# Block sums of the down weights: GpSimd adds in SBUF in place of transfers in DRAM, and two products of a quarter exchanged

## The chip, the core and the metric

One core of a Trainium2 chip runs the whole program. The metric is the device time of one execution in microseconds, taken as the median of three runs. TensorE does the matmuls, VectorE and ScalarE the elementwise work, GpSimd some elementwise work and some transfers, and SyncE issues most loads.

## The reference

A decoder trunk of two layers on 512 tokens of width 1024, in float32. Layer A has sparse attention with compressed, selected and windowed branches and a cross-attention to 256 memory rows; layer B has dilated window attention over keys and values made once from layer A's output, and the same cross-attention. Each layer ends in an MLP, and it is in the two MLPs that the change lies:

```python
def squared_relu_mlp(h, w_up, w_down):            # (512,1024) x (1024,4096) x (4096,1024)
    return jnp.square(jax.nn.relu(h @ w_up)) @ w_down
...
y = y + squared_relu_mlp(rmsnorm(y, mlp_norm[l]), w_up[l], w_down[l])
```

## The kernel before

**Number format.** Every weight block is loaded into a buffer `st` (three of them, 128x1024) and split into a high and a low part in a buffer `w` (four of them): ScalarE copies the high part, VectorE subtracts it from the block. `mm3` then multiplies in three matmuls: high by high, high by low, low by high. `wload` is load and split together.

**The MLP.** `mlp(l)` is called for layer A (l = 0) and layer B (l = 1). The 4096 hidden columns are worked in four quarters `q` of eight 128-column tiles. In the up part, tile by tile, a weight tile is loaded and split, 24 matmuls of 512 columns make the hidden tile in PSUM, ScalarE takes relu and square, and the result is split into `a[j]`. After every second tile `combos` makes, on VectorE, sums and differences of the two tiles' row halves. In the down part the quarter's product with `w_down` is done in seven products in place of eight, by a scheme of block sums (two row halves, two halves of the hidden columns, two column halves of 512). A quarter of `w_down` has four blocks `B[0]` to `B[3]`, each of two half blocks of 128x1024. The products need these stationary sides and weights, in this order:

- X: `a[0..3]`, first rows, with `B[0]`; the sum over quarters of X is kept in `G`.
- Z: a combination, with `T[1]` = B1 + B3; then `into` adds it to the output rows.
- Y: `s2`, with `T[2]` = B0 + B1 + B3; added to `G`.
- Z again, accumulated in the same PSUM banks: `a[4..7]`, last rows, with `T[3]` = B0 + B1 + B2 + B3; `into`.
- V: `s1`, with `T[0]` = B0 + B1; `into`.
- X again, accumulated: `a[4..7]`, first rows, with `B[2]`; `into`.
- V again, accumulated: `s4`, with `B[3]`; `into`.

Each product fills two PSUM banks, in 24 matmuls: for each half block h, six into bank 0, then six into bank 1. `into` reads both banks on VectorE (one operation each), scales by the row's norm factor and adds to the output tile `xn`.

**The sums.** `T[0..3]` lie in DRAM. `blocks` is a generator whose steps issue, for one quarter after the other, four copies of blocks to DRAM tiles from ScalarE's queue, and four accumulating transfers on top of them from GpSimd's queue:

```python
for o, i in ((0, 0), (1, 1), (2, 3), (3, 2)):
    self.behind(self.nc.scalar.dma_start(t[o], b[i]))
    yield
for o, x in ((0, b[1]), (1, b[3]), (2, t[0]), (3, t[2])):
    self.behind(self.nc.gpsimd.dma_start(t[o], x, accum_op=ALU.add, max_dma_last_dim=4096))
```

`behind` makes each of them wait for an earlier marked operation, so that it does not start too soon. The steps for the first quarter are taken during layer A's attention (`paced`, one step every 13 ticks, from the twelfth item on); those of each later quarter during the up part of the quarter before it (`PM`). `product` then loads the half blocks of the sums like any other weight.

**Order.** The program is written as one stream; the framework lists the instructions of every engine in an order that it works out itself from when their inputs and buffers should be ready, and each engine then runs its list in order. A buffer that is taken again waits for the last reader of what it held.

At the end of layer A's MLP (`q` = 3, l = 0) `done` and `columns` square and transpose finished parts of the output while the last products run, and layer B starts with the projection to shared keys and values.

Of the kernel before, what the change touches and what calls it, by code (L numbers as in the profile page):

```python
# [14 lines left out]
P = 128  # L15
# [39 lines left out]


PA = 13
PM = (0, 0, 1, 1, 2, 3, 4, 6)
# [72 lines left out]
def paced(gen, n):  # L131

    while True:
        for _ in range(n):
            yield
        next(gen, None)


# [39 lines left out]
class K:  # L178
    def __init__(self, ctx, tc, ins, out):
        self.tc, self.nc, self.ins, self.out = tc, tc.nc, ins, out  # L180
        ps = lambda n, b: ctx.enter_context(tc.tile_pool(name=n, bufs=b, space=bass.MemoryType.PSUM))
        sb = lambda n, b: ctx.enter_context(tc.tile_pool(name=n, bufs=b))
        self.pacc, self.pS, self.pT, self.pO = ps("acc", 2), ps("ps", 3), ps("pt", 2), ps("po", 1)
        self.one = sb("one", 1)
        self.sb = sb("sb", 1)
        self.dram = ctx.enter_context(tc.tile_pool(name="dram", bufs=1, space=bass.MemoryType.DRAM))
        self.n = 0
        self.ev = 3
        self.staged = []
        self.sums, self.marks = {}, []  # L190
        self.adds, self.far = self.blocks(), 5
        self.lab = "s"
# [3 lines left out]
        cs=2, stt=4, vcb=1, ab=1,  # L196
# [13 lines left out]

    def marked(self, f):

        return lambda *a, **k: self.marks.append(f(*a, **k))  # L213
# [432 lines left out]
    def soft(self, Sp, nb, n):  # L646

        nc = self.nc
        nm = self.t("nm", [P, nb])
        sm = self.t("su", [P, nb])  # L650
        nc.vector.tensor_reduce(out=nm, in_=Sp, axis=AX.X, op=ALU.max, negate=True)
        p = self.t("p2", [P, nb, n])
        for b in range(nb):
            self.marked(nc.scalar.activation)(
                p[:, b, :], Sp[:, b, :], AF.Exp, bias=nm[:, b : b + 1], accum_out=sm[:, b : b + 1]
            )
        return p, sm
# [43 lines left out]
    def layer_a(self):  # L701
# [52 lines left out]
        slow = Work()  # L754
        slow.add(paced(self.adds, PA), None, lambda: len(seen) >= 12)
        attend(items, work, slow, RA, seen)
# [128 lines left out]
    def cmp_scores(self, g, q4, cmp, gt):  # L885
# [4 lines left out]
        VCB = self.t("vcb", [P, 2, P])  # L890
# [45 lines left out]
    def attn_a(self, g, ga, gt, cmp, out):  # L936
# [20 lines left out]
        def front(pr, half, hp, ii):  # L957
# [31 lines left out]
            for br in range(2):  # L989
                self.marked(nc.scalar.activation)(p[br], Sb[br], AF.Exp, bias=nms[br], accum_out=sm[:, br : br + 1])  # L990
# [81 lines left out]
    def behind(self, i):  # L1072

        self.tc.add_manual_dep(
            i.ins, self.marks[-self.far].ins.name, mybir.DependencyInfo(mybir.DependencyClass.Sync, mybir.DependencyReason.DATA),
            reason="start of a transfer",
        )

    def blocks(self):


        for l in range(2):
            for q in range(4):
                b = [self.ins["w_db"][l, q, i].rearrange("h p c -> (h p) c") for i in range(4)]
                t = [self.dram.tile([2 * P, D], F32, name=f"sum{l}{q}_{i}") for i in range(4)]
                for o, i in ((0, 0), (1, 1), (2, 3), (3, 2)):
                    self.behind(self.nc.scalar.dma_start(t[o], b[i]))
                    yield
                for o, x in ((0, b[1]), (1, b[3]), (2, t[0]), (3, t[2])):
                    self.behind(self.nc.gpsimd.dma_start(t[o], x, accum_op=ALU.add, max_dma_last_dim=4096))  # L1090
                    if o == 3:
                        self.sums[l, q] = t
                    yield
# [24 lines left out]
    def mlp(self, l):  # L1118
# [5 lines left out]
        self.far = 1  # L1124
# [74 lines left out]
        for q in range(4):  # L1199
            a, A12, A4 = [None] * 8, [], []  # L1200
            for n in range(8):
# [12 lines left out]
                self.marked(nc.scalar.activation)(u, ps, AF.Relu)  # L1214
# [12 lines left out]
                for _ in range(PM.count(n)):  # L1227
                    next(self.adds, None)

            def product(banks, stat, wsrc, again=False):  # L1230

                for h in range(2):
                    w = self.wload(wsrc[h])
                    for u in range(2):
                        for i in range(2):
# [5 lines left out]
                            )  # L1241
            blk = lambda k0, c0: lambda k: [a[k + k0][:, z, c0 : c0 + H] for z in (0, 1)]
# [3 lines left out]
            B = [ins["w_db"][l, q, i] for i in range(4)]  # L1246
            while (l, q) not in self.sums:
                next(self.adds)
            T = [t.rearrange("(h p) c -> h p c", h=2) for t in self.sums[l, q]]
            two = lambda pool: [self.ps(pool, [P, S]) for _ in range(2)]  # L1250

            def into(src, rows, cols, neg=False):

                for u in range(2):
                    b = 2 * rows + u
                    o = xn[b][:, cols * 512 : (cols + 1) * 512]
                    self.marked(nc.vector.scalar_tensor_tensor)(
# [6 lines left out]
            product(X, blk(0, 0), B[0])  # L1264
# [17 lines left out]
            product(Z, blk(4, H), T[3], True)  # L1282
# [4 lines left out]
            product(V, s1, T[0])  # L1287
# [16 lines left out]
            if last:  # L1304
                done(0, 1)
                if l == 0:
                    columns(0, 1)
# [121 lines left out]
    def attn_b(self, sp, q4, kv, oT, side):  # L1429
# [6 lines left out]
        def front(s, w, ih):  # L1436
# [43 lines left out]
            for ii in range(2):  # L1480
                n = sizes[ii]
                self.marked(nc.scalar.activation)(
# [241 lines left out]
```

## Time and profile before

| | |
|---|---|
| time, median of 3 runs | 1336.94 us (1335.43 to 1343.63) |
| the profiled execution | 1338.41 us, its span 1336.6 us |
| busy: TensorE, its weight loads | 1270.1 us (95%), 1044.9 us (78%) |
| busy: VectorE, ScalarE, GpSimd | 861.6 (64%), 774.7 (58%), 378.2 us (28%) |
| instructions | 18572 |
| moved by DMA | 214.23 MB, mean 160 GB/s |
| accumulating transfers from GpSimd | 32 of 1024 KB, medians 13.5 and 9.6 us to landing |
| mean granted TensorE clock | 0.981 of 2.4 GHz |

The span runs from the first to the last instruction of the profiled execution. Busy time counts an instruction from its start to its end; matmuls are pipelined and overlap, so a TensorE that is busy all the time is one that never stood without a matmul in flight.

### The profile page before, as it was taken

The page shows a single profiled execution, that of the slowest core. Times are in us where ns is not written, and L with a number is a line of the kernel's source. Part 1 is how long each engine was busy: PE and PEld are TensorE (multiplying, and loading weights), DVE is VectorE, ACT ScalarE, POOL GpSimd, SP SyncE. Part 2 cuts the span into 40 slices and gives each one's busy share as a digit, 9 for nine tenths or more (in the row PEclk, how much of TensorE's full clock was granted, in tenths as well). Part 3 has the DMA queues.
Part 4 walks back from the last instruction along what each step waited for, and adds up shares of the span by engine and source line. Part 5 has one row for each costly group of instructions (what it writes and reads, how often), then busy time and mean ns, then how long its engine had stood idle before and what let it go on. Part 6 is the DMA issues. An engine that isn't in the chain of part 4 may idle for free.

```text
span 1336.6 us, 18572 instructions
## 1 busy us (share of the span) xinstructions
PE 1270.1 (95%) x6465; PEld 1044.9 (78%) x6465; DVE 861.6 (64%) x1599; ACT 774.7 (58%) x1709; POOL 378.2 (28%) x481
## 2 busy tenths in 40 slices
PE   8868999999999999999999989989899999999998
PEld 6757787667688888888887878877668888888887
DVE  5976677755366756557478567666666655747556
ACT  6755467686376445463557547766757546455452
POOL 2444584554231000010001878572424001000000
PEclk9887999999999999999998999999999999999999
DMA  7224122333369688796976241211228879798534
GB/s 235 79 88 144 54 74 96 87 75 85 111 198 260 213 278 238 239 245 225 277 211 202 79 131 48 64 40 44 79 87 248 237 223 265 223 273 233 157 110 157
DMA packets 61261, 214.23 MB, mean 160 GB/s; under 512 B 6672, under 2 KB 13840, under 8 KB 60656
## 3 DMA queue, kind: packets, MB, share of 16 engines
q1 hardware_dynamic: 50224, 142.67, 32.8%
q0 software_dynamic: 9344, 35.77, 13.6%
q10 hardware_dynamic: 1600, 34.61, 7.2%
q8 instruction: 51, 0.84, 0.2%
q14 instruction: 42, 0.34, 0.1%
HBM read 207.78 MB, written 72.35 MB: 210 GB/s over the span
## 4 chain that ended last, share of the span: by engine, by line
PE 76%; DVE 8%; ACT 7%; DMA 4%; issue 3%; POOL 1%; ACTq 0%; SPq 0%; POOLq 0%; DVEq 0%
PE s_ps L250 14%; PE s_ps L252 14%; PE s_ps L251 13%; PE s_acc L250 5%; PE s_acc L251 5%; PE s_acc L252 5%; PE s_pt L252 3%; PE s_pt L251 3%; PE s_pt L250 3%; PE s_po L1030 2%; DMA s_st<-in_w_ao_dram 2%; ACT s_p L213 2%; ACT s_w L243 2%; DVE s_w L245 1%; DMA s_st<-in_w_ag_dram 1%
## 5 line engine op out<-in xcount | busy, mean ns | idle before, releaser
L245 DVE TENSOR_TENSOR s_w<-s_st,s_w 128x1024 fp32r<-128x1024 f32 (+3 forms) x240 | 285.4, 1193 | 274.2 <-ACT s_w L243 273.3
L243 ACT ACTIVATE s_w<-s_st 128x1024 fp32r<-128x1024 f32 (+4 forms) x272 | 263.5, 973 | 212.9 <-PE s_pt L252 51.7
L250 PE MATMUL s_ps<-s_act,s_w 128*128 128x512 f32 x576 | 225.4, 393 | 1.1 <-ACT s_act L285 0.7
L252 PE MATMUL s_ps<-s_act,s_w 128*128 128x512 f32 x576 | 225.0, 391 | 0.0
L251 PE MATMUL s_ps<-s_act,s_w 128*128 128x512 f32 x576 | 224.9, 390 | 0.0
L250 PEld LDWEIGHTS s_ps<-s_act,s_w 128*128 128x128 f32 x576 | 108.0, 188 | 25.9 <-ACT s_act L285 1.6
L252 PEld LDWEIGHTS s_ps<-s_act,s_w 128*128 128x128 f32 x576 | 108.1, 188 | 23.8 <-issue 1.6
L251 PEld LDWEIGHTS s_ps<-s_act,s_w 128*128 128x128 f32 x576 | 108.1, 188 | 23.1 <-issue 0.8
L250 PE MATMUL s_acc<-s_w,s_act 128*128 128x512 f32 (+3 forms) x304 | 110.3, 366 | 12.7 <-ACT s_w L243 9.0
L251 PE MATMUL s_acc<-s_w,s_act 128*128 128x512 f32 (+3 forms) x304 | 109.4, 360 | 1.4 <-DVE s_w L245 1.3
L252 PE MATMUL s_acc<-s_w,s_act 128*128 128x512 f32 (+3 forms) x304 | 106.9, 356 | 0.0
L213 ACT ACTIVATE s_p<-s_ps 128x512 f32<-128x512 f32 x64 | 38.2, 597 | 110.9 <-PE s_ps L252 110.9
L1090 POOL DMA_DIRECT2D sum<-in_w_db_dram x16 | 14.4, 900 | 302.6 <-ACT s_p L213 299.1
L660 POOL TENSOR_SCALAR s_p<-s_p,s_cr 128x256 f32<-128x256 f32 (+3 forms) x128 | 69.9, 568 | 89.7 <-DVE s_cr L601 24.1
L250 PEld LDWEIGHTS s_acc<-s_w,s_act 128*128 128x128 f32 x304 | 59.0, 195 | 20.8 <-ACT s_w L243 9.3
L245 POOL TENSOR_TENSOR s_w<-s_st,s_w 128x512 fp32r<-128x512 f32 (+4 forms) x32 | 53.2, 1666 | 74.9 <-ACT s_w L243 74.9
L213 ACT ACTIVATE s_p<-s_ps,s_nm 128x256 f32<-128x256 f32 (+3 forms) x128 | 65.4, 521 | 8.2 <-DVE s_nm L972 3.8
L251 PEld LDWEIGHTS s_acc<-s_w,s_act 128*128 128x128 f32 x304 | 59.0, 194 | 7.4 <-DVE s_w L245 3.1
L252 PEld LDWEIGHTS s_acc<-s_w,s_act 128*128 128x128 f32 x304 | 58.9, 194 | 4.5 <-issue 0.2
L668 ACT ACTIVATE s_pt<-s_pt 128x512 f32<-128x512 f32 (+2 forms) x101 | 52.4, 526 | 15.4 <-PE s_pt L1011 5.7
L285 ACT ACTIVATE s_qk<-s_p 128x256 fp32r<-128x256 f32 (+1 forms) x96 | 46.9, 489 | 23.1 <-DVE s_p L1100 21.1
L1090 POOL DMA_DIRECT2D sum<-sum x16 | 14.1, 882 | 140.6 <-issue 43.4
(334 smaller groups left out, 2971.2 us busy)
## 6 DMA issues: line engine op xcount, KB each, us to landing
s_st<-in_w_up_dram SPq DMA_DIRECT2D x64, 512.0 KB, 4.1
s_st<-sum SPq DMA_DIRECT2D x64, 512.0 KB, 6.2
s_st<-in_w_db_dram SPq DMA_DIRECT2D x48, 512.0 KB, 4.4
sum<-in_w_db_dram POOLq DMA_DIRECT2D x16, 1024.0 KB, 13.5
sum<-sum POOLq DMA_DIRECT2D x16, 1024.0 KB, 9.6
s_st<-in_w_bq_dram SPq DMA_DIRECT2D x16, 384.0 KB, 3.2
s_st<-in_w_ag_dram SPq DMA_DIRECT2D x11, 512.0 KB, 4.4
s_st<-in_w_c_dram SPq DMA_DIRECT2D x8, 512.0 KB, 4.0
```

The source lines that it names most:

```text
L213: return lambda *a, **k: self.marks.append(f(*a, **k))
L243: nc.scalar.activation(w[:, 0], st, AF.Copy)
L245: e.tensor_tensor(out=w[:, 1], in0=st, in1=w[:, 0], op=ALU.subtract)
L250: mm(ps, lh[0], rh[0], start=start, stop=False, skip_group_check=again)
L251: mm(ps, lh[0], rh[1], start=False, stop=False, skip_group_check=again)
L252: mm(ps, lh[1], rh[0], start=False, stop=stop, skip_group_check=again)
L285: nc.scalar.activation(dst[:, 0], src, AF.Copy)
L660: self.nc.gpsimd.tensor_scalar(out=p, in0=p, scalar1=c, scalar2=1.0, op0=ALU.mult, op1=ALU.mult)
L668: self.nc.scalar.activation(dst, src, AF.Copy)
L1030: nc.tensor.matmul(O[x * 64 : x * 64 + 64, q0 + o : q0 + 256], v[:, j, br, :], st[x][br][:, j, o:256], start=half == 0 and br == 0 and j = ...
L1090: self.behind(self.nc.gpsimd.dma_start(t[o], x, accum_op=ALU.add, max_dma_last_dim=4096))
```

## The change

The sums are made in SBUF. At the start of a quarter block 1 is loaded as four 128x512 tiles `U`. After the sixth and seventh hidden tile GpSimd adds block 3, loaded into `st`, to `U` and puts the result into four tiles `T` (buffers named `x`). Then, with the products: `w11` loads and splits block 0 for the first product, and GpSimd adds block 0 to `U` in place; `w3` splits `T` for Z, and GpSimd adds block 0 to `T`; `w2` splits `T` for Y, and GpSimd adds block 2, loaded for it, to `T`; `w4` and `w1` split `T` and `U`; the last two products load blocks 3 and 2 again. A split of `T` or `U` is made in two pieces of 512 columns (`wpieces`), where one of 1024 was made. The DRAM tiles, their transfers, the marks and the pacing go. The last two products change places: V again (`s4` with block 3) comes before X again (block 2), and with them their `into`, `done` and `columns`. A small tile of the attention (`vcb`, one buffer) takes a buffer of the tag `ki` (two).

```diff
-    def behind(self, i):
...
-    def blocks(self):
...
+    def addto(self, out, a, b):
+
+        for i, (o, x) in enumerate(zip(out, a)):
+            self.nc.gpsimd.tensor_tensor(out=o, in0=x, in1=b[:, i * 512 : (i + 1) * 512], op=ALU.add)
+
+    def wpieces(self, t):
+
+        w = self.t("w", [P, 2, 2 * 512], F32R)
+        for i in range(2):
+            self.wsplit(w[:, :, i * 512 : (i + 1) * 512], t[i], "v")
+        return w
...
+            B = [ins["w_db"][l, q, i] for i in range(4)]
+            U, T = [], []
             for n in range(8):
...
-                for _ in range(PM.count(n)):
-                    next(self.adds, None)
...
+                if n < 2:
+
+                    for i in range(2):
+                        U.append(self.t(("qki", "tq")[i], [P, 512]))
+                        nc.sync.dma_start(U[-1], B[1][n][:, i * 512 : (i + 1) * 512])
+                if n in (5, 6):
+
+                    t = [self.t("x", [P, 512]) for _ in range(2)]
+                    self.addto(t, U[2 * n - 10 : 2 * n - 8], self.wdma(B[3][n - 5]))
+                    T += t
...
+            b11 = []
+
+            def w11(h):
+
+                st = self.wdma(B[0][h])
+                b11.append(st)
+                w = self.t("w", [P, 2, 2 * 512], F32R)
+                self.wsplit(w, st, "v")
+                u = U[2 * h : 2 * h + 2]
+                self.addto(u, u, st)
+                return w
+
+            def w3(h):
+
+                t = T[2 * h : 2 * h + 2]
+                w = self.wpieces(t)
+                self.addto(t, t, b11[h])
+                return w
+
+            def w2(h):
+
+                t = T[2 * h : 2 * h + 2]
+                w = self.wpieces(t)
+                self.addto(t, t, self.wdma(B[2][h]))
+                return w
+
+            w4 = lambda h: self.wpieces(T[2 * h : 2 * h + 2])
+            w1 = lambda h: self.wpieces(U[2 * h : 2 * h + 2])
+            w21 = lambda h: self.wload(B[2][h])
+            w22 = lambda h: self.wload(B[3][h])
...
-            product(X, blk(0, 0), B[0])
+            product(X, blk(0, 0), w11)
...
-            product(Z, blk(0, H), T[1])
+            product(Z, blk(0, H), w3)
...
-            product(Y, s2, T[2])
+            product(Y, s2, w2)
...
-            product(Z, blk(4, H), T[3], True)
+            product(Z, blk(4, H), w4, True)
...
-            product(V, s1, T[0])
+            product(V, s1, w1)
...
-            product(X, blk(4, 0), B[2], True)
+            product(V, s4, w22, True)
             if last and l == 0:
                 columns(1, 1)
                 columns_end(1)
+            into(V, 0, 1)
+            if last:
+                done(0, 1)
+            product(X, blk(4, 0), w21, True)
+            if last and l == 0:
+                columns(0, 1)
             into(X, 0, 0)
...
-            product(V, s4, B[3], True)
-            if last and l == 0:
-                columns(0, 0)
-            into(V, 0, 1)
...
```

## Rows read from the trace of the kernel before

**Rows 1.** Stages: window, length, PE, PEld, DVE, ACT, POOL busy (x), clock, DMA share, GB/s.

```profile
150.00:320.00 170.00, 159.50 (x1007) 125.83 (x1007) 119.09 (x318) 122.59 (x370) 99.01 (x139) 1.00 0.29 81
...
362.00:690.00 328.00, 328.00 (x1464) 269.98 (x1463) 202.37 (x292) 175.19 (x258) 28.50 (x27) 1.00 0.81 238
690.00:730.00 40.00, 36.98 (x167) 30.23 (x166) 37.04 (x70) 27.67 (x59) 0.00 (x0) 0.91 0.69 221
```

**Rows 2.** TensorE in order of time, first matmuls of X and of X again.

```profile
512.42 0.39 PE L250 MATMUL s_acc<-s_w,s_qk 128*128 128x512 f32 x1
...
539.62 0.39 PE L250 MATMUL s_acc<-s_w,s_qk 128*128 128x512 f32 x1
```

**Rows 3.** Waits of one quarter's products: total us, times, longest.

```profile
ACT s_w L243 <- PE s_pt L252: 9.0, 6, 1.7
...
ACT s_w L243 <- DMA s_st<-sum: 3.0, 1, 3.0
```

**Rows 4.** VectorE by line and form, the products of one quarter.

```profile
L245 DVE TENSOR_TENSOR s_w<-s_st,s_w 128x1024 fp32r<-128x1024 f32 x14 | 17.0, 1222 | 12.4 <-ACT s_w L243 12.3
L213 DVE SCALAR_TENSOR_TENSOR s_pt<-s_pt,r,s_pt 128x512 f32<-128x512 f32 x4 | 2.8, 742 | 0.0
...
L1100 DVE TENSOR_TENSOR s_p<-s_p,s_p 128x256 f32<-128x256 f32 x3 | 1.3, 418 | 0.0
```

**Rows 5.** VectorE in order of time, the same quarter.

```profile
514.20 1.23 DVE L245 TENSOR_TENSOR s_w<-s_st,s_w 128x1024 fp32r<-128x1024 f32 x1 [3.88 <-ACT s_w L243]
...
523.94 1.22 DVE L245 TENSOR_TENSOR s_w<-s_st,s_w 128x1024 fp32r<-128x1024 f32 x1 [1.84 <-ACT s_w L243]
...
526.40 2.35 DVE L245 TENSOR_TENSOR s_w<-s_st,s_w 128x1024 fp32r<-128x1024 f32 x2
...
538.19 1.23 DVE L245 TENSOR_TENSOR s_w<-s_st,s_w 128x1024 fp32r<-128x1024 f32 x1 [1.46 <-ACT s_w L243]
539.33 1.40 DVE L213 SCALAR_TENSOR_TENSOR s_pt<-s_pt,r,s_pt 128x512 f32<-128x512 f32 x2
```

**Rows 6.** Issues for the sums: queue, count, min/median/max ns.

```profile
L1087 ACTq DMA_DIRECT2D sum<-in_w_db_dram x32: 496/497/610, 159.5 to 1181.7; - x32
...
L1090 POOL DMA_DIRECT2D sum<-sum x16: 869/878/930, 287.6 to 1214.6; - x16
```

**Rows 7.** GpSimd in order of time, late in attention A.

```profile
321.29 0.91 POOL L1090 DMA_DIRECT2D sum<-sum  x1
321.93 1.24 POOL L660 TENSOR_SCALAR s_p<-s_p,s_cr 128x256 f32<-128x256 f32 x2
```

**Rows 8.** Line 441, the adds of squares: min/median/max ns.

```profile
L441 POOL TENSOR_TENSOR s_raw<-s_raw,s_p x14: 1288/1351/2210, 392.7 to 1021.8; 128x512 f32<-128x512 f32 x14
L441 DVE TENSOR_TENSOR s_raw<-s_raw,s_p x7: 684/686/689, 11.4 to 22.6; 128x512 f32<-128x512 f32 x7
```

**Rows 9.** GpSimd in order of time, first MLP.

```profile
392.71 11.48 POOL L441 TENSOR_TENSOR s_raw<-s_raw,s_p 128x512 f32<-128x512 f32 x7
```

**Rows 10.** VectorE in order of time, the same stretch.

```profile
401.54 1.51 DVE L1100 TENSOR_TENSOR s_p<-s_p 128x256 f32<-128x256 f32 x1
...
405.00 0.41 DVE L1100 TENSOR_TENSOR s_p<-s_p,s_p 128x256 f32<-128x256 f32 x1
```

**Rows 11.** All engines in order of time, attention A.

```profile
162.66 1.23 DVE L245 TENSOR_TENSOR s_w<-s_st,s_w 128x1024 fp32r<-128x1024 f32 x1 [0.75 <-ACT s_w L243]
162.68 1.66 POOL L503 TENSOR_TENSOR s_tq<-s_tq,s_rb 128x192 f32<-128x192 f32 x1
...
164.00 0.55 DVE L984 TENSOR_REDUCE s_nm<-s_ps 128x1 f32<-128x384 f32 x1
...
164.30 0.60 POOL L504 TENSOR_TENSOR s_tq<-s_tq,s_rb 128x192 f32<-128x192 f32 x1
```

**Rows 12.** Busy time by stage, end of the first MLP; columns as in rows 1.

```profile
714.00:718.00 4.00, 2.57 (x16) 2.00 (x14) 3.73 (x9) 3.97 (x10) 0.00 (x0) 1.00 0.95 309
718.00:722.00 4.00, 2.41 (x9) 1.93 (x10) 4.00 (x7) 4.00 (x10) 0.00 (x0) 0.60 0.61 192
```

More of the change, by code (lines that the diff above doesn't have):

```diff
@@ L128, in __init__ @@
         self.front, self.back, self.args, self.seg, self.need = front, back, args, seg, need
[L131 to L136, printed above, removed]
 def attend(items, work, side, ratios, seen, lag=1):
@@ L189, in __init__ @@
         self.staged = []
-        self.sums, self.marks = {}, []
-        self.adds, self.far = self.blocks(), 5
         self.lab = "s"
@@ L195 @@
         act=12, st=3, w=4, qk=8, pt4=4, p2=6, raw=2, tmp=4, sq=1, rb=1, tq=2, qki=2, ki=2, x=8, r1=1, r2=1, r3=1, r4=2, r5=2, r6=3, r7=2, nm=6, su=5, cr=6, c1=2, c2=2, nb=4,
-        cs=2, stt=4, vcb=1, ab=1,
+        cs=2, stt=4, ab=1,
     )
@@ L753, in layer_a @@
         items = spread(L[0], C[0], 8, 0) + spread(L[1], C[1], 1, 1) + spread(L[2], C[2], 1, 1) + M
-        slow = Work()
-        slow.add(paced(self.adds, PA), None, lambda: len(seen) >= 12)
-        attend(items, work, slow, RA, seen)
+        attend(items, work, Work(), RA, seen)
         while work.step() is not END:
@@ L889, in cmp_scores @@
         KC, vc = cmp["KC"], cmp["vc"]
-        VCB = self.t("vcb", [P, 2, P])
+        VCB = self.t("ki", [P, 2, P])
         nc.gpsimd.memset(VCB, 0.0)
@@ L1069, in outpart @@
             nc.vector.tensor_tensor(out=self.x[m], in0=ps, in1=xo, op=ALU.add)
-    def behind(self, i):
[L1074 to L1077, printed above, removed]
-    def blocks(self):
[L1082 to L1093, printed above, removed]
+    def addto(self, out, a, b):
[6 more added lines that the diff above has]
+        return w
     def combos(self, u1, u2, a1):
@@ L1226, in mlp, with product @@
                     r, nr = inverse()
-                for _ in range(PM.count(n)):
-                    next(self.adds, None)
-            def product(banks, stat, wsrc, again=False):
+                if n < 2:
[6 more added lines that the diff above has]
+                    T += t
+            def product(banks, stat, weights, again=False):
                 for h in range(2):
-                    w = self.wload(wsrc[h])
+                    w = weights(h)
                     for u in range(2):
@@ L1245, in mlp @@
             s4 = lambda k: [A4[k][:, z] for z in (0, 1)]
[L1246 to L1249, printed above, removed]
             two = lambda pool: [self.ps(pool, [P, S]) for _ in range(2)]
@@ L1299, in mlp @@
                 done(0, 0)
-            product(V, s4, B[3], True)
-            if last and l == 0:
-                columns(0, 0)
-            into(V, 0, 1)
-            if last:
-                done(0, 1)
                 if l == 0:
-                    columns(0, 1)
+                    columns(0, 0)
                     columns_end(0)
```

15 lines of the change are left out of this document (5 added, 10 removed).

## The prediction

> **What bounds the kernel now.** I read the totals of the page first (TensorE is the busiest engine by far), then busy time by stage, then one quarter of an MLP instruction by instruction. By stage [rows 1], the first MLP from 362 to 690 us has TensorE busy 328.00 of 328 us at granted clock 1.00, with the DMA engines at 0.81; the attention stretch from 150 to 320 us leaves TensorE 10.5 us idle, and the join of the first MLP to layer B (690 to 730) leaves 3.0 us. So in an MLP the end is set by the matmuls alone. Five products there take 539.62 - 512.42 = 27.20 us [rows 2], 5.44 each, 24 matmuls at 0.2267 us. A quarter has 8 x 24 + 7 x 24 = 360 of them, 81.6 us; eight quarters are 653 us, half of the kernel. The change keeps every one of these matmuls. It can therefore win only outside the MLPs, and it can lose wherever TensorE is made to wait.
>
> What protects TensorE now is prefetch: the split of a block (a copy on ScalarE, a subtract on VectorE) waits mostly for a free w buffer, that is for TensorE itself (9.0 us in total), and only once for a sum from DRAM (3.0 us), which TensorE did not feel [rows 3]. With four w buffers the split for half-product k may start when k-4 ends. Count halves of 2.72 us from 512.42: half 6 (first half of the fourth product) is due at 512.42 + 16.32 = 528.74, and its subtract begins at 523.94 and takes 1.22, so it is 3.6 us early; half 7 is due at 531.46, its subtract ends about 527.6, 3.9 us early [rows 4, 5].
>
> **What is removed.** Per quarter four DRAM copies issued by ScalarE (0.50 us of its queue each) and four accumulating transfers issued by GpSimd (0.88 each) [rows 6], the loads of four sums (eight half blocks) and all of that traffic. In the MLPs this is worth nothing: TensorE never waits there [rows 1], so the DMA relief only lengthens the lead of the loads. The first quarter's sums are issued inside attention A: four issues on each queue, at most 4 x 0.50 + 4 x 0.9 = 5.6 us of queue time that exponentials or scalings of p could wait behind. One of the GpSimd issues visibly stands in front of the scaling of a block of p (321.29, then the scaling at 321.93) [rows 7]. Bound 0 to -5.6 us; I take -2, about a third, since both engines also idle in that stretch.
>
> **Loads.** SyncE now issues 12 half blocks a quarter where it issued 14: block 1 as four loads of half the size, then blocks 3, 0, 2, 3, 2. Two of the three st buffers hold block 0 until it has been added to T, and the third holds block 2, so the loads for the last two products queue on SyncE behind those adds. The tenth half is due at 512.42 + 27.2 = 539.6, far behind adds that should end near 525: cost nothing, covered by two products of TensorE. Buffers named ki in place of vcb: nothing, one memset.
>
> **The adds.** Each quarter has 16 adds of 128x512 on GpSimd. The same operation stands in the trace: 1.29 us at least, 1.35 median, against 0.686 on VectorE [rows 8]; seven in a row took 11.48 us, 1.64 each, with VectorE at work [rows 9]. 16 x 1.35 = 21.6 us fits in 81.6. The price is on VectorE: while GpSimd adds, a VectorE operation on two SBUF inputs waits for the add in progress. A 128x256 subtract takes 1.51 us in that run and 0.41 after it [rows 10], +1.1 each; in the other direction a 1024-wide subtract holds an add until it ends (a 192-wide add took 1.66, the next one 0.60), while a VectorE read of PSUM beside GpSimd keeps its usual time [rows 11]. The Trainium skill says the same (GPSIMD Engine Reference, § 1 Specifications: the SBUF interfaces are shared, with contention for VectorE instructions with two SBUF inputs), and its § 4.1 Engine selection advises against GpSimd for two-input elementwise work. The trace agrees on both; taken as a rule on this change, it is the second case below.
>
> Ten of the 16 adds (B1+B3, block 0 into U, and block 0 into the first half of T) fall in the up part or in the 3.88 us that VectorE idles ahead of 514.20 [rows 5]; there a w serves 24 matmuls, 5.44 us, and the delay is covered: nothing. The other six follow one another between 514.2 and 527.6: T+B0 for the second half, then T+B2 for both. Each needs the split of the old T by ScalarE and VectorE, and the next split needs the add. VectorE has in that stretch five subtracts of 1.22 and the combos (0.42 each) [rows 4], all on two SBUF inputs. Middle: six adds delay VectorE by 1.1 each, 6.6; less its idle of 1.84 in front of 523.94 [rows 5] and the 3.9 of lead, 0.9 us of waiting for TensorE per quarter. Lower bound 0 (the adds meet the PSUM reads instead: the adds of G and the into operations). Upper bound: each add costs its whole 1.35, so 8.1 - 1.84 - 3.9 = 2.4. I take the middle, since the 1.1 was measured on these very shapes: 8 x 0.9 = +7.2 us, bounds 0 to +19. Splitting T in two 512-wide pieces adds a fixed part of about 0.14 per half, inside that bound.
>
> **The exchange.** V = s1 product is now followed at once by the s4 product into the same two PSUM banks, so its first matmul waits until VectorE has read bank 0; before, the X product lay between. In the trace the V product ends at 539.62 [rows 2]. VectorE is then in the subtract that began at 538.19, and the two reads follow from 539.33, 1.40 for both [rows 5], 0.742 for one [rows 4]: bank 0 is free at 540.07, 0.45 late. Bank 1 is free at 540.73 and needed at 539.62 + 0.45 + 1.36 = 541.4: no second wait. Queued behind the reads on VectorE is the next subtract, which has 3 us of lead. 8 x 0.45 = +3.6 us; bounds 0 (the read goes ahead of the subtract) and 0.8 (the subtract begins just before), so 0 to +6.4. At the end of the first MLP, where VectorE is busy 37.04 of 40 us [rows 1], it may be 1 us more; the order of the last columns only changes places.
>
> **Sum.** -2 + 7.2 + 3.6 = +8.8. The profiled execution took 1338.41 us (span 1336.6 and 1.8 around it), 1.5 above the median of the three runs, 1336.94. 1338.41 + 8.8 = 1347.2; on the median 1345.7, so I say 1346.
>
> **The cases.** A change of less than 1% (13.4 us) is what a measurement of this kernel can hardly tell from none.
> - Forecast, 0.50: short waits in the products, 1338 to 1350.
> - The exclusion of GpSimd and VectorE sets the pace, 0.30: the chain split, add, split falls behind in every quarter. It decides once the quarter waits more than (13.4 + 2) / 8 = 1.9 us. At 2.4 + 0.45 it gives 8 x 2.85 - 2 = +20.8, 1358. For it: VectorE and the adds together have little idle in that stretch, and VectorE runs in order, so a piece that queues behind combos delays its add too. Against it: 3.6 to 3.9 us of lead. A lower clock could add to it: after TensorE had been busy only 2.57 of 4 us and then 2.41, the granted clock was 0.60 [rows 12]; waits of one microsecond did not bring that about inside an MLP, which shows none, so this stays unpriced beyond the range.
> - The adds hide completely and attention gains, 0.17: 1336.94 - 5.6 + 0 to 3.6, so 1331 to 1338. For it: VectorE is busy 202.37 of 328 us in the MLP [rows 1]. Against it: the reads at 539.33.
> - The instruction lists come out in another order, so that the adds to U fall into the product stretch too, and the change does not take the sums off the path: 4 x 1.35 more there, which is the second case and is in its chance.
> - Faster by over 1%, 0.03: it would need more than all of the 10.5 us idle in attention A.
>
> The bounds reach from 1336.94 - 5.6 = 1331 to 1336.94 + 19 + 6.4 = 1362; less the outer tenth on either side, 1333 to 1359. Slower by over 1%: 0.30; faster: 0.03; within: 0.67.
>
> **What would show it.** Right: in the MLP stages TensorE busy below the stage's length, its waits put down to VectorE's subtract (or ScalarE's copy) of w in the third and fourth product, and to the reads of V once a quarter; 256-wide VectorE operations of 1.5 us beside GpSimd adds; the quarter 82.5 to 83.5 us long. Wrong: a quarter of 81.6 us (the adds hidden, and the read ahead of the subtract), or waits of several microseconds at one place, above all for a load behind a held st buffer. A longer or shorter attention stage by more than 5 us would mean that the order of its instructions changed, which I have not priced.

## The result and the profile after

The changed kernel takes 1352.9 us (median of 4 executions, 1349.32 to 1357.2) beside 1336.87 for the kernel before: ratio 1.0111, 95% interval 1.0066 to 1.0156. The forecast was 1346 with a range of 1333 to 1359. So the time lies inside the range, above the likeliest case (1338 to 1350), and its median is just past the 1% that I had called hardly measurable, in the part that had 0.30. The profiled execution took 1349.32 us (span 1347.2).

Where the time went is read from stage lengths. A quarter of an MLP begins with the first Relu on ScalarE; the difference of two such starts is the length of a quarter. First quarter of the first MLP, in ScalarE's order of time, kernel before:

```profile
390.83 0.60 ACT L213 ACTIVATE s_p<-s_ps 128x512 f32<-128x512 f32 x1 [0.33 <-PE s_ps L252]
...
474.54 0.60 ACT L213 ACTIVATE s_p<-s_ps 128x512 f32<-128x512 f32 x1 [4.38 <-PE s_ps L252]
```

and after (line numbers have moved: the Relu is L1184, the split of a block L225 on ScalarE and L227 on VectorE, the split of activations L267 and L270, the combos L1069, the new adds L1055, reads of a product L1262, a product's three matmuls L232 to L234):

```profile
391.28 0.60 ACT L1184 ACTIVATE s_p<-s_ps 128x512 f32<-128x512 f32 x1 [0.33 <-PE s_ps L234]
...
479.07 0.60 ACT L1184 ACTIVATE s_p<-s_ps 128x512 f32<-128x512 f32 x1 [4.37 <-PE s_ps L234]
```

That quarter took 83.71 before and 87.79 after. In this way for all stages (us; A is from the start to the first Relu of the first MLP, B from its last quarter's first Relu through layer B to the second MLP's, so that the first MLP's last quarter lies in B; q0 to q2 are the first three quarters, of the first and then of the second MLP; "end" is the last quarter to the end of the span, which is read to 0.1 us; below the first row stand the differences to it, of one profiled execution each):

| kernel | A | q0 | q1 | q2 | B | q0 | q1 | q2 | end |
|---|---|---|---|---|---|---|---|---|---|
| before | 390.83 | 83.71 | 81.60 | 81.60 | 372.06 | 83.71 | 81.60 | 81.60 | 79.89 |
| after | +0.45 | +4.08 | +0.23 | +0.24 | -1.66 | +3.29 | +0.19 | +0.18 | +3.60 |
| e1 exchange alone | -1.34 | 0 | 0 | 0 | +4.59 | -0.01 | 0 | 0 | +0.26 |
| e2 no adds | +2.18 | -0.01 | 0 | 0 | +1.18 | 0 | 0 | 0 | +0.25 |
| e3 adds on VectorE | +1.33 | 0 | +0.89 | +1.06 | +4.73 | -0.01 | +1.04 | +1.02 | +4.34 |
| e4 before plus adds | -2.08 | +4.15 | +2.80 | +2.80 | +5.01 | +4.28 | +3.74 | +3.44 | +1.26 |
| e5 old order | +3.89 | +4.18 | +0.23 | +0.23 | +3.72 | +3.26 | +0.22 | +0.19 | +0.18 |
| e6 fewer held loads | +0.04 | +2.72 | +3.88 | +4.03 | +6.49 | +2.55 | +3.15 | +3.90 | +6.04 |
| e7 squares on VectorE | +1.24 | -0.12 | +0.22 | +0.23 | +3.37 | -0.11 | +0.19 | +0.20 | +3.58 |
| e8 no sums in attention | +4.04 | -0.01 | 0 | 0 | -4.61 | 0 | 0 | 0 | +0.28 |
| e9 e5 and e7 | +3.51 | -0.11 | +0.21 | +0.19 | +2.41 | -0.11 | +0.19 | +0.20 | +0.21 |
| e10 before, squares | +2.48 | -0.11 | 0 | 0 | -0.55 | -0.12 | 0 | 0 | 0 |
| e11 before again | -0.82 | -0.01 | 0 | 0 | -3.50 | 0 | 0 | 0 | +0.03 |
| e12 after again | +0.46 | +4.00 | +0.23 | +0.23 | +0.20 | +3.17 | +0.20 | +0.19 | +5.02 |

In the columns of quarters and the end the changed kernel loses 11.8 us in all, and 11.0 of it in three: the first of each MLP and the very last. The middle ones, where I had placed 1.35 each, lose 0.2. The row of "before again" says how the table is to be read: the quarters repeat within 0.03 us, A and B do not.

The stage of the first MLP in the view of busy time (length, then PE, PEld, DVE, ACT, POOL busy, granted clock, DMA share, GB/s; it answers to [rows 1]):

```profile
362.00:690.00 328.00, 326.02 (x1444) 267.02 (x1443) 241.31 (x311) 175.08 (x282) 111.96 (x71) 0.99 0.38 123
```

DMA fell from 0.81 to 0.38, and TensorE, which had no idle time, was idle 1.98 us. VectorE is busy 38.9 us longer, though it was given no add. The groups of that stage show on what (line, form, count, busy and mean ns, idle before):

```profile
L227 DVE TENSOR_TENSOR s_w<-s_st,s_w 128x1024 fp32r<-128x1024 f32 x52 | 67.1, 1291 | 65.4 <-ACT s_w L225 65.3
L227 DVE TENSOR_TENSOR s_w<-s_x,s_w 128x512 fp32r<-128x512 f32 x48 | 45.9, 991 | 4.5 <-ACT s_w L225 4.4
...
L270 DVE TENSOR_TENSOR s_qk<-s_p,s_qk 128x256 fp32r<-128x256 f32 x32 | 26.4, 825 | 5.3 <-ACT s_qk L267 5.3
...
L1262 DVE SCALAR_TENSOR_TENSOR s_pt<-s_ps,n,s_pt 128x512 f32<-128x512 f32 x8 | 5.9, 739 | 0.0
```

Subtracts on two SBUF inputs have grown (a 512-wide one takes 991 ns in the mean and 0.68 us where GpSimd rests, below; a 256-wide one 825), reads of PSUM have kept their time (739, beside 742 in [rows 4]). GpSimd's adds on their side take longer than the 1351 of [rows 8]:

```profile
L1055 POOL TENSOR_TENSOR s_x<-s_x,s_st x64: 1288/1677/2609, 435.0 to 1316.8; 128x512 f32<-128x512 f32 x64
```

Last, TensorE's waits in the two MLPs (engine, waiting and awaited tile, total us, times, longest): first from 391 to 715, then from 1000 to the end. The kernel before has no row in either.

```profile
PE s_ps L232 <- ACT s_qk L267: 2.0, 1, 2.0
PE s_acc L233 <- DVE s_w L227: 0.9, 1, 0.9
...
PE s_acc L233 <- DVE s_w L227: 3.0, 1, 3.0
PE s_ps L232 <- ACT s_qk L267: 1.3, 1, 1.3
```

**The first quarter.** GpSimd, in order of time:

```profile
395.92 8.72 POOL L423 TENSOR_TENSOR s_raw<-s_raw,s_p 128x512 f32<-128x512 f32 x5
404.58 1.49 POOL L1055 TENSOR_TENSOR s_x<-s_qki,s_st 128x512 f32<-128x512 f32 x1
...
409.15 1.48 POOL L1055 TENSOR_TENSOR s_x<-s_tq,s_st 128x512 f32<-128x512 f32 x1
422.09 1.30 POOL L1055 TENSOR_TENSOR s_qki<-s_qki,s_st 128x512 f32<-128x512 f32 x1 [11.46 <-DMA s_st<-in_w_db_dram]
```

The squares' adds, which stood there before [rows 9], are followed at once by four new ones, so GpSimd is at work without a break to 410.6. VectorE beside it, and then ScalarE:

```profile
403.41 1.50 DVE L1069 TENSOR_TENSOR s_p<-s_p,s_p 128x256 f32<-128x256 f32 x1
...
409.39 2.32 DVE L227 TENSOR_TENSOR s_w<-s_st,s_w 128x1024 fp32r<-128x1024 f32 x1
411.63 0.68 DVE L270 TENSOR_TENSOR s_act<-s_p,s_act 128x512 fp32r<-128x512 f32 x1
412.24 0.41 DVE L270 TENSOR_TENSOR s_x<-s_p,s_x 128x256 fp32r<-128x256 f32 x1
...
434.23 4.69 DVE L227 TENSOR_TENSOR s_w<-s_x,s_w 128x512 fp32r<-128x512 f32 x4
438.84 1.51 DVE L1069 TENSOR_TENSOR s_p<-s_p,s_p 128x256 f32<-128x256 f32 x1
```

```profile
415.99 1.06 ACT L225 ACTIVATE s_w<-s_st 128x1024 fp32r<-128x1024 f32 x1 [5.05 <-DMA s_st<-in_w_up_dram]
...
441.78 0.42 ACT L267 ACTIVATE s_qk<-s_p 128x256 fp32r<-128x256 f32 x1 [4.98 <-DVE s_p L1069]
```

A 256-wide operation takes 1.50 to the end of the adds and 0.41 after it; the subtract that frees a load buffer ends only at 411.7, SyncE issues the next up tile's load right then, and ScalarE waits 5.05 us for it.

```profile
411.74 0.33 SPq L213 DMA_DIRECT2D s_st<-in_w_up_dram  x1
```

From there the rest of the up part runs 2 to 6 us late (by the Relus) into the adds of T; VectorE's combos at the end of the up part (438.84) stand behind four splits that share their time with those adds (4.69 for four, 1.17 each), ScalarE waits 4.98 for the combos, and TensorE 1.98 for ScalarE at 442.25. Its clock falls right behind that (TensorE busy and granted clock are the second and the seventh value; 0.50 is the 1.2 GHz level of 2.4):

```profile
440.00:442.00 2.00, 0.27 (x2) 0.00 (x0) 2.00 (x3) 0.22 (x1) 1.46 (x2) 1.00 0.53 193
442.00:444.00 2.00, 1.75 (x6) 1.27 (x7) 2.00 (x6) 2.00 (x6) 0.00 (x0) 0.85 0.68 229
444.00:446.00 2.00, 2.00 (x7) 1.52 (x6) 1.91 (x4) 2.00 (x5) 1.97 (x1) 0.50 0.09 37
446.00:448.00 2.00, 2.00 (x9) 1.59 (x8) 2.00 (x2) 0.70 (x2) 2.00 (x2) 0.79 0.04 8
```

Two us times 0.15, 0.50 and 0.21 of missing clock are 1.72; with the wait 3.7 of the quarter's 4.08. The fall of the clock is not what makes the loss, though: in e5, which differs only in the last two products of a quarter, the clock stays at 1.00 there, two more waits come instead, and the loss is 4.18. Its waits from 391 to 715 us:

```profile
PE s_ps L232 <- ACT s_qk L267: 2.2, 1, 2.2
PE s_pt L233 <- DVE s_w L227: 0.6, 1, 0.6
PE s_ps L233 <- DVE s_w L227: 0.3, 1, 0.3
```

In the second MLP's first quarter too there are three waits, of 1.28, 0.60 and 0.37, and the clock stays at 1.00; they are 2.25 of its 3.29.

**The last quarter.** VectorE is busy without a gap from 1304 to 1332 (4.00 of every 4 us): three pairs of reads of G are due there, as before, and the pieces of T and U beside the adds. TensorE waits once:

```profile
1328.77 0.39 PE L234 MATMUL s_pt<-s_w,s_act 128*128 128x512 f32 x1
1328.99 0.61 PE L232 MATMUL s_acc<-s_w,s_qk 128*128 128x512 f32 x2
1332.62 0.50 PE L233 MATMUL s_acc<-s_w,s_qk 128*128 128x512 f32 x1 [3.01 <-DVE s_w L227]
```

s_acc is X, s_pt is V: behind V's first product TensorE goes to the first half of X again, not to V again as the new code reads. TensorE's order in the trace is V, first half of X again, V again, second half of X again; the awaited w is the third that VectorE makes, after both halves for V again. VectorE:

```profile
1327.76 1.22 DVE L227 TENSOR_TENSOR s_w<-s_st,s_w 128x1024 fp32r<-128x1024 f32 x1
1328.90 1.40 DVE L1262 SCALAR_TENSOR_TENSOR s_pt<-s_ps,r,s_pt 128x512 f32<-128x512 f32 x2
1330.22 2.35 DVE L227 TENSOR_TENSOR s_w<-s_st,s_w 128x1024 fp32r<-128x1024 f32 x2
```

The weights are split in the order of the code, the products are done in another, and VectorE has no time in hand: the half that is needed first comes third.

### The profile page after: what moved, and what is told of

Same layout as the page of the kernel before. It is cut to its first block, busy times and chain, and to the rows that moved or that the text cites. A ratio compares the mean times of both kernels' runs of the same rounds, so it can differ in the third digit from the quotient of the medians.

```text
span 1347.2 us, 18692 instructions
## 1 busy us (share of the span) xinstructions
PE 1272.3 (94%) x6465; PEld 1042.3 (77%) x6465; DVE 954.3 (71%) x1663; ACT 781.5 (58%) x1773; POOL 557.4 (41%) x577
## 3 DMA queue, kind: packets, MB, share of 16 engines
HBM read 132.28 MB, written 5.24 MB: 102 GB/s over the span
## 4 chain that ended last, share of the span: by engine, by line
PE 70%; DVE 15%; ACT 7%; DMA 4%; issue 3%; POOL 1%; SPq 0%; ACTq 0%; DVEq 0%; POOLq 0%
PE s_ps L233 12%; PE s_ps L232 12%; PE s_ps L234 12%; PE s_acc L232 5%; PE s_acc L233 5%; PE s_acc L234 5%; DVE s_w L227 5%; PE s_pt L232 2%; PE s_pt L234 2%; PE s_pt L233 2%; PE s_po L1010 2%; ACT s_w L225 2%; DVE s_p L1069 2%; DVE s_pt L1262 1%; PE s_ps L961 1%
## 5 line engine op out<-in xcount | busy, mean ns | idle before, releaser
L227 DVE TENSOR_TENSOR s_w<-s_st,s_w 128x1024 fp32r<-128x1024 f32 (+3 forms) x176 | 212.7, 1212 | 160.5 <-ACT s_w L225 159.8
L225 ACT ACTIVATE s_w<-s_st 128x1024 fp32r<-128x1024 f32 (+4 forms) x208 | 195.8, 946 | 160.3 <-PE s_pt L234 36.2
L232 PE MATMUL s_ps<-s_act,s_w 128*128 128x512 f32 x576 | 225.3, 393 | 0.7 <-ACT s_act L267 0.7
L234 PE MATMUL s_ps<-s_act,s_w 128*128 128x512 f32 x576 | 224.9, 391 | 0.0
L1055 POOL TENSOR_TENSOR s_x<-s_x,s_st 128x512 f32<-128x512 f32 x64 | 103.3, 1633 | 92.4 <-DVE s_w L227 92.4
L232 PEld LDWEIGHTS s_ps<-s_act,s_w 128*128 128x128 f32 x576 | 108.0, 188 | 25.2 <-ACT s_act L267 1.6
L234 PEld LDWEIGHTS s_ps<-s_act,s_w 128*128 128x128 f32 x576 | 108.2, 188 | 23.8 <-issue 1.6
L232 PE MATMUL s_acc<-s_w,s_act 128*128 128x512 f32 (+3 forms) x304 | 110.2, 365 | 13.2 <-ACT s_w L225 8.8
L1055 POOL TENSOR_TENSOR s_x<-s_qki,s_st 128x512 f32<-128x512 f32 x16 | 26.2, 1638 | 212.5 <-DMA s_st<-in_w_db_dram 193.3
L234 PE MATMUL s_acc<-s_w,s_act 128*128 128x512 f32 (+3 forms) x304 | 107.0, 356 | 0.0
L227 DVE TENSOR_TENSOR s_w<-s_x,s_w 128x512 fp32r<-128x512 f32 x96 | 91.9, 991 | 9.0 <-ACT s_w L225 8.8
L1184 ACT ACTIVATE s_p<-s_ps 128x512 f32<-128x512 f32 x64 | 38.0, 594 | 85.7 <-PE s_ps L234 85.7
L227 POOL TENSOR_TENSOR s_w<-s_st,s_w 128x512 fp32r<-128x512 f32 (+4 forms) x32 | 54.4, 1702 | 75.6 <-ACT s_w L225 69.3
L270 DVE TENSOR_TENSOR s_qk<-s_p,s_qk 128x256 fp32r<-128x256 f32 (+1 forms) x96 | 76.8, 800 | 10.4 <-ACT s_qk L267 10.4
L267 ACT ACTIVATE s_qk<-s_p 128x256 fp32r<-128x256 f32 (+1 forms) x96 | 47.0, 490 | 60.3 <-DVE s_p L1069 58.2
L225 ACT ACTIVATE s_w<-s_x 128x512 fp32r<-128x512 f32 x96 | 57.5, 623 | 37.8 <-POOL s_x L1055 37.8
L232 PEld LDWEIGHTS s_acc<-s_w,s_act 128*128 128x128 f32 x304 | 58.4, 193 | 21.0 <-ACT s_w L225 9.3
```

The lines of the kernel that those rows point to most:

```text
L225: nc.scalar.activation(w[:, 0], st, AF.Copy)
L227: e.tensor_tensor(out=w[:, 1], in0=st, in1=w[:, 0], op=ALU.subtract)
L232: mm(ps, lh[0], rh[0], start=start, stop=False, skip_group_check=again)
L234: mm(ps, lh[1], rh[0], start=False, stop=stop, skip_group_check=again)
L267: nc.scalar.activation(dst[:, 0], src, AF.Copy)
L270: nc.vector.tensor_tensor(out=dst[:, 1], in0=src, in1=dst[:, 0], op=ALU.subtract)
```

## The experiments

Theories after the result: **A**, GpSimd's adds and VectorE's operations on two SBUF inputs exclude one another, and it shows where VectorE is late; **B**, held load buffers delay the loads; **C**, the exchange costs; **D**, the smaller pieces and other lists cost.

**e1**: the kernel before with the last two products (and their reads and columns) exchanged.

```
-            product(X, blk(4, 0), B[2], True)
+            product(V, s4, B[3], True)
...
-            product(V, s4, B[3], True)
+            product(X, blk(4, 0), B[2], True)
```

> The kernel before with nothing changed but the order of the last two products. Theory A (the price of the change is GpSimd's adds, which keep VectorE off its two-input operations): 1335 to 1339 us, since the profile after shows X's first half listed between V and V again, so that no wait on the reads of V is left. Rival C (the exchange costs what I forecast or more): 1340 to 1350.

1342.77 us, ratio 1.0045 (1.0029 to 1.0062). The time lies in rival C's range, but not for the reason that I had priced: no quarter in a column is longer, the end by 0.26, and the wait of 0.45 a quarter on the reads of V does not exist. Of the 5.7 us of the median 5.4 lie in A and B (see e10, e11 and what stays open).

**e2**: the change without its adds.

```
-            self.nc.gpsimd.tensor_tensor(out=o, in0=x, in1=b[:, i * 512 : (i + 1) * 512], op=ALU.add)
+            pass
...
-                    self.addto(t, U[2 * n - 10 : 2 * n - 8], self.wdma(B[3][n - 5]))
+                        nc.sync.dma_start(t[i], B[3][n - 5][:, i * 512 : (i + 1) * 512])
...
-                self.addto(t, t, self.wdma(B[2][h]))
```

> The changed kernel without any of the 16 adds a quarter: T holds block 3 alone, loaded straight into its tiles, U holds block 1; the sums of the computation are left out. Pieces, exchange and loads of blocks stay (block 2 is loaded once less). Theory A: 1333 to 1339, all of the loss gone. Rival C or a rival D (the splits in pieces, the other order of instructions): 1345 to 1353 still.

1338.49 us, ratio 1.0009 (0.9995 to 1.0023), quarters as before, VectorE busy 204.88 of the 328 us. All that the quarters lose comes with the adds. D is out as a cause by itself; the exchange is in e2 as well, so it costs the quarters nothing without the adds.

**e3**: the adds on VectorE.

```
-            self.nc.gpsimd.tensor_tensor(out=o, in0=x, in1=b[:, i * 512 : (i + 1) * 512], op=ALU.add)
+            self.nc.vector.tensor_tensor(out=o, in0=x, in1=b[:, i * 512 : (i + 1) * 512], op=ALU.add)
```

> The changed kernel with its adds on VectorE, 0.69 us each in place of 1.3 to 1.7 on GpSimd; the same buffers are held, but for a shorter time. Theory A says that an add costs VectorE up to 1.1 us while it runs on GpSimd, so 0.69 on its own queue is no worse: 1338 to 1350. If it is VectorE's mere load that counts, with little exclusion, 16 x 0.69 = 11 us more a quarter: above 1356.

1353.4 us, ratio 1.0132 (1.011 to 1.0154), between the two ranges expected: no better, but elsewhere. First quarters 0, middle ones +1.0, the last +4.34. What the adds cost VectorE is read over the first MLP's three whole quarters, which hold 48 adds; e2 (no adds), the change (adds on GpSimd), e3 (adds on VectorE):

```profile
393.01:639.91 246.90, 246.90 (x1102) 204.69 (x1101) 156.21 (x241) 132.43 (x212) 11.63 (x8) 1.00 0.35 115
391.28:642.74 251.46, 249.48 (x1102) 205.51 (x1101) 190.04 (x241) 132.32 (x213) 89.75 (x56) 0.99 0.39 125
392.16:641.02 248.86, 247.66 (x1102) 204.61 (x1101) 182.29 (x289) 134.40 (x212) 11.63 (x8) 1.00 0.41 126
```

48 adds done by GpSimd keep VectorE busy 33.8 us longer (190.04 less 156.21, with the same 241 operations), done by VectorE itself 26.1.

**e4**: the kernel before with 16 idle adds a quarter on GpSimd, behind the splits of up tiles 6 and 7 and of the first three products.

```
+                    nc.gpsimd.tensor_tensor(
+                        out=self.t("qki", [P, 512]), in0=w[:, 0, c].bitcast(F32), in1=w[:, 1, c].bitcast(F32), op=ALU.add
+                    )
```

> The kernel before, sums still made by transfers in DRAM, with 16 adds a quarter on GpSimd whose results nobody needs, after the splits of the sixth and seventh up tile and of the first three products; they read w, which is held anyway. Theory A: 1343 to 1353. Rival B (the price of the change is in the loads: st buffers held until an add is done make later loads late): 1336 to 1339.

1363.8 us, ratio 1.0209 (1.0189 to 1.0228), above the range that I had given theory A: 2.8 to 4.3 more in every quarter but the last, though nobody waits for an add's result and no load buffer is held by one. The adds do hold the w that they read, but ScalarE, which fills w, is listed in neither MLP as waiting for GpSimd to give one back. A is enough for losses of this size, and their place decides the size: these adds cost a middle quarter 2.8 to 3.7, the change's own 0.2.

**e5**: the change with the last two products in the old order (e1's diff the other way round).

> The changed kernel with the last two products of each quarter in the old order (X between the two products of V); the adds stay. If the exchange costs what it cost alone (+5.7 us of the median, all of it outside the quarters, at the join of the first MLP to layer B and in layer B): about 1347, the quarters unchanged against the changed kernel. If the loss is the adds' alone and the stages outside the MLPs only scatter: 1353 within 3 us. If my priced wait of 0.45 us a quarter were there: each middle quarter 0.45 shorter than in the changed kernel.

1350.89 us, ratio 1.0099 (1.0068 to 1.0131). The time does not tell the first two cases apart; the stages do. The end of it loses 0.18 instead of 3.60, the rest of the quarters is unchanged. VectorE's list at that place is the same, row for row in length, and it is as full; TensorE no longer waits:

```profile
1336.67 1.22 DVE L227 TENSOR_TENSOR s_w<-s_st,s_w 128x1024 fp32r<-128x1024 f32 x1
1337.81 1.40 DVE L1262 SCALAR_TENSOR_TENSOR s_pt<-s_ps,r,s_pt 128x512 f32<-128x512 f32 x2
1339.13 2.35 DVE L227 TENSOR_TENSOR s_w<-s_st,s_w 128x1024 fp32r<-128x1024 f32 x2
```

```profile
1337.67 0.39 PE L234 MATMUL s_pt<-s_w,s_act 128*128 128x512 f32 x1
1337.90 0.62 PE L232 MATMUL s_acc<-s_w,s_qk 128*128 128x512 f32 x2
1338.36 0.39 PE L233 MATMUL s_acc<-s_w,s_qk 128*128 128x512 f32 x1
```

The split at 1336.67 is now the one that X again needs. So the last quarter's loss is the exchange and the adds together: with either alone it is 0.26 (e1) and 0.18.

**e6**: the load buffers held shorter.

```
-                    self.addto(t, U[2 * n - 10 : 2 * n - 8], self.wdma(B[3][n - 5]))
+                        nc.sync.dma_start(t[i], B[3][n - 5][:, i * 512 : (i + 1) * 512])
+                        nc.gpsimd.tensor_tensor(out=t[i], in0=t[i], in1=U[2 * n - 10 + i], op=ALU.add)
...
-                self.addto(t, t, b11[h])
+                self.addto(t, t, self.wdma(B[0][h]))
```

> The changed kernel with the load buffers held shorter: the two halves of block 3 are loaded straight into T and U is added in place (same 16 adds), and block 0 is loaded a second time for its add to T instead of being held since its split. If held buffers and late loads are the cause (an up tile's load waits for the adds to end in the first quarter): the first quarters lose under 1 us, where the changed kernel loses 4.1 and 3.3, and the time is 1345 or less. If the cause is that GpSimd's adds and VectorE's operations on two SBUF inputs exclude one another: first quarters still +3 to +4, 1353 within 3 us, and the last quarter the same or later.

1370.85 us, ratio 1.026 (1.0228 to 1.0291). The time is over both ranges expected. The first quarters still lose 2.6, the middle ones now 3 to 4. Its TensorE waits from 391 to 715 us:

```profile
PE s_pt L233 <- DVE s_w L227: 4.3, 6, 0.9
PE s_ps L233 <- DVE s_w L227: 3.7, 4, 1.0
```

Many short waits for a split, where the change has one of 2.0 and one of 0.9. The late load is gone: the up tile's split that starts at 415.99 in the change, after 5.05 us of waiting, starts at 409.80 here, as in the kernel before (409.76). But the adds stand elsewhere too, and the loss comes from other waits, so e6 does not decide between A and B for the first quarter; e7 does. Adds at another place are dearer; what sets them back in e6 (the second load of block 0, or the order of the new adds) I did not take apart.

**e7**: the change with the squares' adds of the first quarters on VectorE.

```
-                self.square(k, x[k])
+                self.square(k, x[k], nc.vector)
```

> The changed kernel with the sums of squares of the MLP's first quarter added on VectorE instead of GpSimd, so that GpSimd's queue is free for the adds of B1 and B3 at the start of the quarter. If the first quarters lose because GpSimd is already late and at work beside VectorE when the new adds come: first quarters +1 instead of +4.1 and +3.3, about 1347. If held load buffers or the adds as such are the cause: the first quarters stay at +3 to +4, about 1353. If VectorE has no room for 4 us more there: first quarters +5 or more, 1356.

1346.58 us, ratio 1.0078 (1.0048 to 1.0107). The first quarters lose nothing (-0.1); the end is as in the change. VectorE does seven adds more there and is earlier all the same:

```profile
403.13 0.42 DVE L1069 TENSOR_TENSOR s_p<-s_p,s_p 128x256 f32<-128x256 f32 x1
...
405.64 1.23 DVE L227 TENSOR_TENSOR s_w<-s_st,s_w 128x1024 fp32r<-128x1024 f32 x1 [0.23 <-ACT s_w L225]
```

The subtract that frees the buffer is at 405.64 instead of 409.39 and takes 1.23 instead of 2.32, and the load behind it is issued at 406.89 instead of 411.74. Theory B is answered by the same rows: block 3's two buffers are held as long as in the change (the last add that reads them ends at 410.9 here, at 410.6 there), and the quarter loses nothing. Holding them costs nothing by itself; it only puts the next up tile's load (issued at 396.49 in the kernel before) behind VectorE's subtract, so that a late subtract makes it late.

```profile
409.41 1.47 POOL L1055 TENSOR_TENSOR s_x<-s_tq,s_st 128x512 f32<-128x512 f32 x1
```

**e8**: the kernel before without the sums that were issued inside attention A.

```
+                if l + q == 0:
+                    self.sums[0, 0] = None
+                    continue
```

> The kernel before, without the sums of the first quarter of the first MLP, that is without the four copies and four accumulating transfers issued inside attention A (that quarter multiplies plain blocks instead, so its sums are left out). My term for what attention A gains from their removal was -2 us, bounds 0 to -5.6: by it 1335 and a first stage 2 us shorter. If the two queues had idle time enough: the same as before within 1 us, and the first stage within its scatter.

1336.49 beside 1337.47 us, ratio 0.9996 (0.9981 to 1.0011). No gain is seen: A was 4.04 longer in the profiled execution. The interval, down to -2.5 us, does not by itself exclude my -2.

**e9**: e5 and e7 together.

> The changed kernel with the two edits that each took away one loss: the old order of the last two products, and the first quarters' sums of squares on VectorE. If the two losses are separate (GpSimd's queue in the first quarters, the exchange beside a full VectorE in the last one), every quarter is within 0.3 us of the kernel before, the sum of the MLP stages +1.5, and the time 1338 to 1340. If one wait only takes the place of the other, or the rest is the adds' own: a first or last quarter still 2 us or more longer, 1345 or more.

1344.76 us, ratio 1.0041 (1.0027 to 1.0055). Each quarter is within 0.21 of before, 0.78 in all, and no wait of TensorE is listed in either MLP. The quarters are as expected, the time is not: 6.5 us over the kernel before, 5.7 of them in A and B. It is the best of the versions that make the sums in SBUF, and it does not beat the kernel before.

**e10**: the kernel before with e7's edit, a control.

> The kernel before with the first quarters' sums of squares added on VectorE, a control: nothing of the change in it. If moving the squares is worth something by itself: the first quarters shorter than 83.7, and 1335 or less. If it only clears the way for the new adds: no difference, 1337 within 1 us.

1340.44 us, ratio 1.0016 (1.0001 to 1.003): 2 us slower, an interval that only just leaves out no difference, with each quarter the same or 0.1 shorter. So an edit that costs the MLP nothing seems to move the time by 2 us elsewhere.

**e11** and **e12**: the two kernels once more, unedited.

> The kernel before, profiled once more, nothing changed, to see by how much each stage differs between two executions of one program. If the stages outside the MLPs' quarters scatter with the granted clock: the quarters repeat within 0.05 us (83.7, 81.6, 81.6, last one 79.9), while the first stage (390.8) and the stage from the last quarter of the first MLP through layer B (372.1) differ by 2 to 4 us, and the span follows the mean granted clock. If all stages repeat within 0.5 us, then the shifts of up to 5 us that the variants show there are effects of their edits.

> The changed kernel, profiled once more, nothing changed. If its losses in the quarters are what its instructions make and not luck of one execution: +4.1 and +3.3 in the first quarters, +0.2 in the middle ones, +3.6 in the last, repeated within 0.1 us. The rest of its 16 us, about 4, would be in the two stages outside, where it scatters by 2 to 4 us.

1334.08 and 1352.46 us, one execution each. Quarters repeat (within 0.03, and within 0.12 for the change), B differs by 3.5 in the same program. One exception: the end of e12 lost 5.02, not 3.60. It has the same wait of 3.0 us, and then a clock that fell:

```profile
1331.30:1335.30 4.00, 1.00 (x2) 0.83 (x3) 4.00 (x6) 0.56 (x1) 0.00 (x0) 0.86 0.84 258
1335.30:1339.30 4.00, 4.00 (x14) 3.20 (x13) 1.49 (x2) 0.49 (x1) 0.00 (x0) 0.72 0.37 138
```

## Why the prediction was right, and where its steps failed

The sign and the mechanism held (GpSimd's adds at VectorE's cost, short waits of TensorE), and the time lay in the range, which was 26 us wide (by its own rule it begins at 1334 and not 1333). The places did not hold: the middle quarters are nearly the 81.6 us that I had named as a sign of being wrong, and so is a wait of 3.0 us at one place. Term by term:

- **Attention A, -2: no gain seen.** In the nine profiled executions without these transfers (the change, e12, e2, e3 and e5 to e9) A is 0.04 to 4.04 longer than in the first row, never shorter. One issue seen in front of a scaling [rows 7] was no evidence of a path.
- **The adds, +7.2 from the late products of every quarter: wrong place.** The step "the delay is covered: nothing" for the adds of the up part failed in the first quarters, because I looked at one middle quarter and forgot that GpSimd and VectorE start the first one with the squares' adds [rows 9, 10], the very rows from which I took the price. They lose 4.1 and 3.3 there, and nothing in e7, where the squares' adds are out of the way. The step "0.9 per quarter" failed the other way: the lead of [rows 5] covered nearly all of it (0.2). That 4.1 + 3.3 + 4 x 0.2 comes to 8.2, near 7.2, is chance.
- **The exchange, +3.6 from reads of V: 0 of that kind.** V again does not follow V; TensorE's list puts half of X again between, and in e1 no quarter in a column is longer. In its stead came 3.4 us in the last quarter, from a split order that no longer is the order of use, and only because the adds leave VectorE without slack (e5 against the change; e1). That this is near 3.6 is chance too. The last quarter of the first MLP has the same loss, smaller (below).
- **The clock, left unpriced:** the kernel before has no wait in an MLP, so no row stood behind the words on waits of one microsecond. A wait of 2.0 us was followed by granted clock 0.50, one of 2.2 at the same place (e5) was not, and the quarter lost as much; one of 3.0 was followed by no fall in one execution and by a loss of about 1.4 in another.
- **The lists, loads and pieces, taken at nothing:** e2 bears it out in the quarters.

My second case (every quarter waits over 1.9 us) did not happen in the change; it did in e6 and in all but the last quarter of e4, with 16 adds at other places. The sentence on a held st buffer came close: the late load of 415.99 was behind one, but what it waited for was VectorE's late subtract on the third buffer, and in e7 the other two are held as long without a loss.

The Trainium skill (GPSIMD Engine Reference, § 4.1 Engine selection) would put such adds on VectorE, as about twice as fast there. The single add is (0.686 beside 1.351 us, [rows 8]); for the kernel e3 shows no gain: the adds took VectorE 26.1 us instead of 33.8 (48 adds), the first quarters lost nothing and the others more, 8.3 us in all beside 11.8, and the time was the same (1353.4 beside 1352.9).

**What stays open.** The median is 16.0 us up; 11.8 (13.0 in e12) lie in the quarters and in the end, so 3 to 4 in A and B. The variants show the same (the difference of medians less the sum of those columns): 5.4 in e1, 8.0 in e3, 4.3 in e4, 4.9 in e5 and e7, 7.1 in e6, 5.7 in e9, 2.4 in e10, but 1.2 in e2 and -1.3 in e8. A part can be placed, since B holds the last quarter of the first MLP. Its last product matmul, in the kernel before and in the change, with the quarter's first Relu at 637.74 and 642.74:

```profile
715.30 0.39 PE L252 MATMUL s_pt<-s_w,s_x 128*128 128x512 f32 x1
```

```profile
722.88 0.39 PE L234 MATMUL s_acc<-s_w,s_qk 128*128 128x512 f32 x1
```

That is 77.6 us after the Relu before (the same in e8, e10 and e11) and 80.1 in the change (and in e7 and e12), beside 77.8 in e5, 77.5 in e2 and 78.5 in e1: here too the exchange and the adds together cost, 2.6 us. Not all of it goes on into layer B, whose first projection matmul starts 0.5 us later in the change, and 2.0 later in e12 than in e11. For the rest a lower mean granted clock goes with the longer times of some kernels: 0.9773 over e9's 10 executions beside 0.9808 over 21 of the kernel before (0.0035 of 1338 us is 4.7), and 0.9777 over e1's 9 beside 0.9803 over 18. But e2 has 0.9781 with only 1.2 us, and e4 has its 4.3 at 0.9802. In layer B and at the join TensorE has many short waits, and at which of them the clock falls differs between kernels and between executions of one (B: 372.06 and 368.56). Which edit makes that likelier wasn't settled, and so the 5 us that e9 still loses there have no shown cause.

## What to carry to other kernels

An add given to GpSimd is not free for VectorE if VectorE's work is on two SBUF inputs: count it as at least as much VectorE time as doing it there (33.8 us beside 26.1 for 48 adds here), and look for the place where VectorE has no idle time, in the first and the last pass of a loop and not only in a middle one. Before pricing a wait from an order of products, read the order in which the built program lists them on each engine; keep the order in which weights are prepared the order in which they are used. Judge a stage only by stages that repeat: run one program twice and see which do.

## What the runs showed of the hardware

- The exclusion costs both engines: a 256-wide VectorE subtract 0.41 to 1.50 us, a 1024-wide one 1.22 to 2.32, a 128x512 add on GpSimd 1.29 to 2.61; 48 adds on GpSimd kept VectorE busy 33.8 us longer.
- The granted clock fell to 0.50 after one wait of 2.0 us within an MLP, and stayed at 1.00 after one of 2.2 us at the same place in another kernel (e5). In the same place of the second MLP three waits of 0.4 to 1.3 us left it at 1.00.
- Taking away half of the HBM traffic (read 207.78 MB to 132.28, written 72.35 to 5.24) shortened no quarter; with the adds left out as well (e2) the kernel took 1338.49 beside 1337.07 us.
